# Inverting the chunk triangles: substitution down to 16x16 blocks, one more merge level on TensorE, pools in another order

## The chip, the core and the metric

The kernel runs on one core of a Trainium2 chip. The metric is the device time of one execution in microseconds, the median of several runs. One core has five engines that each work through a queue of their own, in order: TensorE (PE, with its weight loads as PEld), VectorE (DVE), ScalarE (ACT), GpSimd (POOL) and SyncE (SP, which here only issues transfers). They meet through semaphores. Transfers between device memory and the core's SBUF go through 16 DMA engines.

## The reference

One layer of a diffusion block over 1024 latent tokens and 256 context tokens, width 1024, all in float32. The part that matters here is the gated delta rule: 4 heads of width 128, both directions in time, in chunks. In each chunk a unit lower triangular system is solved:

```python
A = jnp.where(strict, jnp.einsum('nbhid,nbhjd->nbhij', kb, kc) * decay, 0.0)
rhs = jnp.concatenate([vc * bc[..., None], kb * jnp.exp(G)[..., None]], axis=-1)
sol = lax.linalg.triangular_solve(A + jnp.eye(CHUNK, dtype=A.dtype), rhs,
                                  left_side=True, lower=True, unit_diagonal=True)
u, w = sol[..., :dv], sol[..., dv:]
def step(S, xs):
    u_c, w_c, q_c, qk_c, k_c, gl = xs
    v_new = u_c - jnp.einsum('bhck,bhkv->bhcv', w_c, S)
    o = jnp.einsum('bhck,bhkv->bhcv', q_c, S) + jnp.einsum('bhij,bhjv->bhiv', qk_c, v_new)
    S = gl * S + jnp.einsum('bhck,bhcv->bhkv', k_c, v_new)
    return S, o
```

Around it stand, in this order, the modulated norm, one combined input projection (q, k, v with a short convolution, z, and four groups rq, rk, rv, rg for a second, retention branch of 4 heads with rotary positions), the norms and gates, the output projection, and a SwiGLU of inner width 2816.

## The kernel before

The 1280 tokens are 10 tiles of 128; the kernel takes 128 as the chunk of the delta rule too, so there are 10 tiles x 4 heads x 2 directions = 80 triangles of 128x128. Big products are made in three passes (hi x hi, hi x lo, lo x hi; lines L381 to L383, tile `tm`, 128x256 each). A scheduler fixes the order of every engine's queue ahead of the run; within it, a tile that takes an older tile's place in SBUF waits for that tile's last use. Tiles live in pools that are opened and closed like a stack, so what a pool lies upon depends on the order in which pools are opened.

The stages around the change:

- `token_major` projections of g 6 and 7 (rg) with their weights in pool W2; then R2 and W2 are closed and GP, GU and GI opened.
- `pre(t)` for each tile, in batches `BATCH = [[0,1,2,9],[3,8,4,7],[5,6]]`: on PE kk, the transpose qt and kq; on POOL the differences of decays `e` (L591, L593) and `sp` (L609); on ACT the exponentials (L595, L608); on DVE `ut` (L603) and `sp` (L605). The scaled triangles go out to device memory as `un` (L606), other operands of the scan as `sd` (L610).
- `invert(b)`: loads the 32x32 diagonal blocks of a batch as one row per block (`yr`, L624), copies them to L, straight for one direction on ACT (L631) and transposed for the other on DVE (L632), and inverts all blocks at once by 31 steps of substitution with two DVE operations each (L638, L640). X and its transpose XT (L642) go out as `xd` (L644).
- `solve(0)` and `solve(1)` are pre and invert of batches 0 and 1. Then come the v convolution (`conv_block`), whose result is transposed on PE (vT, L728), scaled on ACT into the only buffer `vt` (L731) and stored (L732), and `pre` of batch 2.
- `merge(b)`: loads U from `un` (L655), puts the inverted blocks over its diagonal blocks from `xd` (L659), and loads the transposed blocks into t64 (L660), which POOL has zeroed (L657). From the 32x32 inverses it makes those of 64 and then of 128 by products of the form -X1 A X2: 32x32 products (L679, L686, L689) with an eviction on DVE (L682) and copies on ACT (L692, L695), then 64x64 ones (L702, L706, L703, L708). The result is stored to `sd` (L710). U has one buffer, so a batch's load waits for the previous batch's store.
- invert(2) stands between merge(0) and merge(1). Beside the merges PE works on `tm` products of the next projections (fill).
- Then the scan, which loads its operands as `pk`; its steps (kS, r, Tr L792, vn, up L799) alternate between the directions. The rotary part of the second branch uses DVE (L398, L401) and POOL (L403).

Of the kernel before, what the change touches and what calls it, by code (L numbers as in the profile page):

```python
# [17 lines left out]
P = 128  # L18
D = 1024
# [18 lines left out]
def build(nc, tc, ap, dbg=None, stop=None, marks=None):  # L38
    root = ExitStack()
    V, S, G, T, SY = nc.vector, nc.scalar, nc.gpsimd, nc.tensor, nc.sync  # L40

    def pool(name, bufs=1, side=None, space=None):
        kw = {}
        if side is not None:
            kw["side"] = side
        if space is not None:
            kw["space"] = space
        if space is not DRAM:
            kw["reuse_waits"] = "tile"
# [8 lines left out]
    def close(p):  # L58
        p_close.pop(id(p)).close()
# [32 lines left out]
    def bank_b(name):  # L92
        return bank("pb", name)
# [67 lines left out]
    try:  # L161

        cc = const("cc", [P, KT, 2])
        ident = const("ident", [P, P])
# [118 lines left out]
        for gi, grp in enumerate(XGROUPS):  # L283
            n, t0 = len(grp), grp[0]
# [8 lines left out]
            sl = slice(t0 * P, (t0 + n) * P)  # L293
# [158 lines left out]
        ps = bank_b("G")  # L452
# [14 lines left out]
        ps = bank_b("GT")  # L467
# [145 lines left out]

        xds = {}

        def invert(b):

            nc_ = len(BATCH[b])
            nu = nc_ * H
            nb = 4 * nu  # L620
            xd = xds[b] = dr.tile([4 * nb, 1024], F32, tag="xd%d" % b, name="xd%d" % b)
            yr = GI.tile([P, 1024], F32, tag="yr", name="yr", bufs=1)
            for k in range(4):
                SY.dma_start(yr[k:2 * nb:4].rearrange("r (i j) -> r i j", j=32),  # L624
                             un[b][q32[k]].rearrange("i e u j -> (e u) i j")[:, :, q32[k]])
            L = GI.tile([P, 1024], F32, tag="L", name="L", bufs=3)
            X = GI.tile([P, 1024], F32, tag="X", name="X", bufs=2)
            G.memset(X, 0.0)
            G.memset(X[:, 0::33], 1.0)
            m = lambda t: t[:2 * nb].rearrange("p (i j) -> p i j", j=32)  # L630
            S.activation(L[:nb], yr[:nb], AF.Copy)  # L631
            V.tensor_copy(m(L)[nb:], yr[nb:2 * nb].rearrange("p (i j) -> p j i", j=32))  # L632
            for j in range(31):
                n = 31 - j
                tmp = GI.tile([P, 256], F32, tag="tmp%d" % b, name="tmp", bufs=2)
                t3 = tmp[:2 * nb, :n * (j + 1)].rearrange("p (i c) -> p i c", c=j + 1)
                sh = [2 * nb, n, j + 1]
                V.tensor_tensor(t3, bc(m(L)[:, j + 1:, j], sh, 2), bc(m(X)[:, j, :j + 1], sh, 1), ALU.mult)  # L638
                xs = m(X)[:, j + 1:, :j + 1]
                V.tensor_tensor(xs, xs, t3, ALU.subtract)  # L640
            XT = GI.tile([P, 1024], F32, tag="L", name="XT", bufs=3)
            V.tensor_copy(m(XT), X[:2 * nb].rearrange("p (i j) -> p j i", j=32))  # L642
            for i, x in enumerate((X[:nb], XT[nb:2 * nb], X[nb:2 * nb], XT[:nb])):
                SY.dma_start(xd[i * nb:(i + 1) * nb], x)  # L644

        def blocks(b):

            nu = len(BATCH[b]) * H
            nb = 4 * nu

            def blk(dram, k):
                return dram.rearrange("(u b) (i j) -> b i u j", b=4, j=32)[k]

            uu = GM.tile([P, 2, len(BATCH[b]), H, P], F32, tag="U", name="U%d" % b, bufs=1)
            SY.dma_start(uu.rearrange("p e c h j -> p e (c h) j"), un[b])  # L655
            tt = GM.tile([P, 2, nu, 64], F32, tag="t64", name="t64", bufs=1)
            G.memset(tt, 0.0)  # L657
            for k in range(4):
                SY.dma_start(uu[q32[k]].rearrange("p e c h j -> p (e c h) j")[:, :, q32[k]], blk(xds[b][:2 * nb], k))  # L659
                SY.dma_start(tt[q32[k]].rearrange("p e u j -> p (e u) j")[:, :, (k % 2) * 32:(k % 2) * 32 + 32],  # L660
                             blk(xds[b][2 * nb:], k))
            return uu, [uu[:, 1 - d] for d in range(2)], [tt[:, d] for d in range(2)]

        def merge(b):

            uu, ub, t64 = blocks(b)
            nu = len(BATCH[b]) * H
            q = q32
            u = [x.rearrange("p c h j -> p (c h) j") for x in ub]
            t = t64  # L670
# [3 lines left out]
            three = lambda ps, sl, w: ps[sl].rearrange("p (n j) -> p n j", j=w)  # L674
            ps1 = bank_b("m1")
            for n in range(nu):
                for d, p, a, bb in pairs:
                    ca = (a % 2) * 32
                    T.matmul(ps1[q[bb], n * 32:n * 32 + 32], u[d][q[a], n, q[bb]], t[d][q[a], n, ca:ca + 32],  # L679
                             start=True, stop=True)  # L680
            xt1 = GM.tile([P, 16, 32], F32, tag="xt1", name="xt1", bufs=1)
            V.tensor_scalar(xt1.rearrange("p n j -> p (n j)")[:, :nu * 32], ps1[:, :nu * 32], -1.0, None, ALU.mult)  # L682
            ps2, ps3 = bank_b("m1"), bank_b("m1")
            for n in range(nu):
                for d, p, a, bb in pairs:
                    T.matmul(ps2[q[a], n * 32:n * 32 + 32], xt1[q[bb], n, :], u[d][q[bb], n, q[bb]],  # L686
                             start=True, stop=True)
                    if p == d:
                        T.matmul(ps3[q[bb], n * 32:n * 32 + 32], u[d][q[bb], n, q[bb]], xt1[q[bb], n, :],  # L689
                                 start=True, stop=True)  # L690
            for d, p, a, bb in pairs:
                S.activation(u[d][q[a], :, q[bb]], three(ps2[:, :nu * 32], q[a], 32), AF.Copy)  # L692
                if p == d:
                    ca = (a % 2) * 32
                    S.activation(t[d][q[bb], :, ca:ca + 32], three(ps3[:, :nu * 32], q[bb], 32), AF.Copy)  # L695
            halves = [(0, slice(0, 64), slice(64, 128)), (1, slice(64, 128), slice(0, 64))]
            for n0 in range(0, nu, 8):
                ps1, ps2 = bank_b("m2"), bank_b("m2")
                xt2 = GM.tile([P, 8, 64], F32, tag="xt2", name="xt2", bufs=1)
                for n in range(8):  # L700
                    for d, A, B in halves:
                        T.matmul(ps1[B, n * 64:n * 64 + 64], u[d][A, n0 + n, B], t[d][A, n0 + n, :], start=True, stop=True)  # L702
                V.tensor_scalar(xt2.rearrange("p n j -> p (n j)"), ps1, -1.0, None, ALU.mult)  # L703
                for n in range(8):
                    for d, A, B in halves:
                        T.matmul(ps2[A, n * 64:n * 64 + 64], xt2[B, n, :], u[d][B, n0 + n, B], start=True, stop=True)  # L706
# [789 lines left out]
```

## Time and profile before

| | us |
|---|---|
| median of 3 runs (lowest, highest) | 1504.32 (1503.76, 1508.56) |
| the profiled execution | 1499.94 |
| its span | 1498.2 |
| PE busy | 1405.7 |
| DVE busy | 978.5 |
| POOL busy | 638.6 |
| ACT busy | 607.0 |

The profile is of one execution. Its rows are read as follows. A row of a group says line, engine, operation, written tile <- read tiles, shapes, the count, then the busy time with the mean of one in ns, then the idle time of the engine just before these instructions with what ended most of it. A row of the timeline says start and duration in us, engine, line and operation, and in brackets the idle time before it with what ended it. In the table by stretches, each engine has its busy time and its count; PEclk is TensorE's granted clock as a share of full speed, the mean of which over this execution was 0.974. The trace keeps two records for one 32x32 product in float32.

### The profile page before, as it was taken

The numbers are of one execution on the slowest core, as the hardware profiler recorded it, in microseconds if no ns is written. First come the engines' busy times: TensorE is split into PE (matmuls) and PEld (weight loads), VectorE is DVE, ScalarE is ACT, GpSimd is POOL, SyncE is SP. The second block draws the span as 40 slices with busy tenths as digits, with TensorE's granted clock in tenths as the row PEclk, the third lists the DMA queues.
The fourth block names the chain that finished last, engine by engine and source line by source line (L and its number), as shares of the span: only waits on it lengthen the run. The fifth ranks groups of instructions, "written<-read, shape, count | busy, mean of one in ns | idle before, by whom it ended". The sixth has DMA issues, their size and how long they took to land.

```text
span 1498.2 us, 24215 instructions
## 1 busy us (share of the span) xinstructions
PE 1405.7 (94%) x8927; PEld 1210.8 (81%) x8927; DVE 978.5 (65%) x1926; ACT 607.0 (41%) x1267; POOL 638.6 (43%) x589
## 2 busy tenths in 40 slices
PE   6899999987898899998799899989999999999997
PEld 2898888976888899988678688878888888788886
DVE  5966695279778345678767786646555555658477
ACT  5733653365451121235544433223333333445445
POOL 0310101387124243224326578989555553325322
PEclk9899999997999999999999999999999999999999
DMA  8555685478597756985742256665222231785863
GB/s 329 197 175 164 207 239 167 143 234 267 147 276 213 227 170 252 370 334 204 246 147 106 86 191 223 240 238 204 105 106 106 106 141 68 237 281 188 295 217 113
DMA packets 171703, 298.16 MB, mean 199 GB/s; under 512 B 43368, under 2 KB 93752, under 8 KB 166208
## 3 DMA queue, kind: packets, MB, share of 16 engines
q1 hardware_dynamic: 119424, 251.07, 48.9%
q10 hardware_dynamic: 49360, 36.88, 8.0%
q0 software_dynamic: 2800, 8.65, 1.6%
q8 instruction: 70, 1.15, 0.3%
q14 instruction: 49, 0.40, 0.1%
HBM read 206.60 MB, written 89.96 MB: 198 GB/s over the span
## 4 chain that ended last, share of the span: by engine, by line
PE 64%; DVE 12%; DMA 10%; POOL 5%; issue 4%; ACT 3%; SPq 1%; ACTq 0%; POOLq 0%; DVEq 0%
PE ffn L1187 8%; PE ffn L1186 8%; PE ffn L1185 8%; PE tm L383 4%; PE tm L382 4%; PE tm L381 4%; PE fo L1313 3%; PE fo L1312 3%; PE fo L1311 3%; PE b L484 2%; PE b L486 2%; PE b L485 2%; PE op L1044 2%; PE op L1046 2%; PE op L1045 2%
## 5 line engine op out<-in xcount | busy, mean ns | idle before, releaser
L381 PE MATMUL tm<-whi,hhi 128*128 128x256 f32 (+1 forms) x704 | 203.9, 292 | 8.7 <-ACT whi L319 4.3
L382 PE MATMUL tm<-wlo,hhi 128*128 128x256 f32 (+1 forms) x704 | 204.5, 292 | 3.1 <-DVE wlo L320 3.1
L383 PE MATMUL tm<-whi,hlo 128*128 128x256 f32 (+1 forms) x704 | 204.4, 293 | 0.0
L381 PEld LDWEIGHTS tm<-whi,hhi 128*128 128x128 f32 x704 | 137.4, 196 | 11.1 <-ACT whi L319 5.4
L382 PEld LDWEIGHTS tm<-wlo,hhi 128*128 128x128 f32 x704 | 138.0, 196 | 5.8 <-DVE wlo L320 3.6
L1185 PE MATMUL ffn<-t,whi 128*128 128x512 f32 x352 | 137.7, 392 | 4.0 <-ACT whi L319 3.0
L383 PEld LDWEIGHTS tm<-whi,hlo 128*128 128x128 f32 x704 | 137.6, 196 | 2.2 <-issue 0.9
L1187 PE MATMUL ffn<-t,wlo 128*128 128x512 f32 x352 | 137.5, 392 | 1.1 <-DVE wlo L320 1.1
L1186 PE MATMUL ffn<-t,whi 128*128 128x512 f32 x352 | 137.8, 392 | 0.5 <-DVE t L1080 0.5
L319 ACT ACTIVATE whi<-wraw 128x512 fp32r<-128x512 f32 (+2 forms) x98 | 75.2, 772 | 132.0 <-PE ffn L1186 77.6
L320 DVE TENSOR_TENSOR wlo<-ws,whi 128x512 fp32r<-128x512 f32 x88 | 94.4, 1073 | 50.1 <-ACT whi L319 50.0
L319 ACT ACTIVATE whi<-ws 128x512 fp32r<-128x512 f32 x88 | 55.6, 631 | 170.6 <-PE ffn L1186 120.1
L320 DVE TENSOR_TENSOR wlo<-wraw,whi 128x512 fp32r<-128x512 f32 (+2 forms) x92 | 100.5, 1094 | 35.6 <-ACT whi L319 35.3
L1312 PE MATMUL fo<-wlo,ahi 128*128 128x512 f32 x308 | 120.0, 390 | 0.8 <-DVE wlo L320 0.8
L1311 PE MATMUL fo<-whi,ahi 128*128 128x512 f32 x308 | 119.3, 390 | 0.7 <-ACT ahi L319 0.7
L1313 PE MATMUL fo<-whi,alo 128*128 128x512 f32 x308 | 118.8, 389 | 0.0
L1185 PE MATMUL ffn<-b,whi 128*128 128x512 f32 x264 | 103.7, 393 | 3.8 <-ACT whi L319 3.8
L1187 PE MATMUL ffn<-b,wlo 128*128 128x512 f32 x264 | 103.7, 393 | 1.6 <-DVE wlo L320 1.6
L1186 PE MATMUL ffn<-b,whi 128*128 128x512 f32 x264 | 103.5, 392 | 0.0
L484 PE MATMUL b<-hhi,whi 128*128 128x512 f32 (+1 forms) x256 | 95.5, 373 | 2.2 <-ACT y L488 2.2
L485 PE MATMUL b<-hlo,whi 128*128 128x512 f32 (+1 forms) x256 | 95.1, 372 | 0.0
L486 PE MATMUL b<-hhi,wlo 128*128 128x512 f32 (+1 forms) x256 | 94.8, 370 | 0.0
(422 smaller groups left out, 3495.3 us busy)
## 6 DMA issues: line engine op xcount, KB each, us to landing
adaw<-ada_w SPq DMA_DIRECT2D x48, 512.0 KB, 5.6
pk<-sd SPq DMA_DIRECT2D x16, 1536.0 KB, 9.7
wraw<-wfi SPq DMA_DIRECT2D x44, 512.0 KB, 3.5
ar<-ad SPq DMA_DIRECT2D x33, 512.0 KB, 6.5
w<-wfo SPq DMA_DIRECT2D x22, 512.0 KB, 3.5
wd<-tw SPq DMA_DIRECT2D x11, 1024.0 KB, 4.8
ad<-act SPq DMA_DIRECT2D x20, 512.0 KB, 4.7
raw<-wd SPq DMA_DIRECT2D x20, 512.0 KB, 5.0
```

The costliest lines, as they stand in the source:

```text
L319: S.activation(hi, raw, AF.Copy)
L320: e.tensor_tensor(lo, raw, hi.bitcast(F32), ALU.subtract)
L381: T.matmul(o, hhi[:, k, tsl], whi[:, k % 4, :], start=(k == 0), stop=False)
L382: T.matmul(o, hhi[:, k, tsl], wlo[:, k % 4, :], start=False, stop=False)
L383: T.matmul(o, hlo[:, k, tsl], whi[:, k % 4, :], start=False, stop=(k == KT - 1))
L484: T.matmul(o, whi[:, k, :], hh, start=(k == 0), stop=False)
L1185: T.matmul(o, whi[:, k, :], xhi(xn, slice(0, 4), k), start=(first and k == 0), stop=False, **kw)
L1186: T.matmul(o, whi[:, k, :], xlo(xn, slice(0, 4), k), start=False, stop=False, **kw)
L1187: T.matmul(o, wlo[:, k, :], xhi(xn, slice(0, 4), k), start=False, stop=(k == 3), **kw)
L1311: T.matmul(po[g][i], ahi[:, ts], whi, start=(j == 0 and not kw), stop=False, **kw)
L1312: T.matmul(po[g][i], ahi[:, ts], wlo, start=False, stop=False, **kw)
L1313: T.matmul(po[g][i], alo[:, ts], whi, start=False, stop=(j == FH - 1), **kw)
```

## The change

Five things are edited.

1. Substitution runs only inside the two 16x16 diagonal blocks of each 32x32 block: 15 steps, each on both blocks at once. Rows of L, X and yr are 1056 long, so that a view `halved` with a stride of 528 reaches both blocks.
2. Each merge begins with a new level from 16 to 32: POOL multiplies the off-diagonal 16x16 blocks into `off`, with a factor `half` (1 or 0 by partition) that keeps only the right rows (L683); PE multiplies `off` with the transposed blocks (L688), ACT evicts with a minus (nw, L691), PE makes the two products for the block and its transpose (L697, L701), and DVE adds them to DT and D (L703, L704). ACT copies the finished 32x32 blocks into U and t64 (L706, L708).
3. The inverted blocks are loaded into tiles of their own, D and DT (L664, L665), no longer over U and t64.
4. `half`, `off` and t64 are made once, ahead of merge(0), not per merge.
5. The pools are opened in the order GI, GU, GP; GP and GU are closed before GM is opened, behind pre of batch 2. Before, GM was opened ahead of that pre, beside all three.

The loads of yr and un, the store of xd and the later merge levels stay; their lines move (L624 to L627, L644 to L649, L655 to L660, L679 to L715, L682 to L718, L792 to L831 and so on).

```diff
+        GI = pool("gi")
+        GU = pool("gu")
         GP = pool("gp")
-        GU = pool("gu")
-        GI = pool("gi")
...
+        halved = lambda x: x.rearrange("p (s y) -> p s y", y=528)[:, :, :512].rearrange("p s (i j) -> p s i j", j=32)[:, :, :, :16]
...
-            S.activation(L[:nb], yr[:nb], AF.Copy)
-            V.tensor_copy(m(L)[nb:], yr[nb:2 * nb].rearrange("p (i j) -> p j i", j=32))
-            for j in range(31):
-                n = 31 - j
-                tmp = GI.tile([P, 256], F32, tag="tmp%d" % b, name="tmp", bufs=2)
-                t3 = tmp[:2 * nb, :n * (j + 1)].rearrange("p (i c) -> p i c", c=j + 1)
-                sh = [2 * nb, n, j + 1]
-                V.tensor_tensor(t3, bc(m(L)[:, j + 1:, j], sh, 2), bc(m(X)[:, j, :j + 1], sh, 1), ALU.mult)
-                xs = m(X)[:, j + 1:, :j + 1]
-                V.tensor_tensor(xs, xs, t3, ALU.subtract)
...
+            S.activation(Lh[:nb], yh[:nb], AF.Copy)
+            V.tensor_copy(Lh[nb:2 * nb], yh[nb:2 * nb].rearrange("p s i j -> p s j i"))
+            Lh, Xh = Lh[:2 * nb], Xh[:2 * nb]
+            for j in range(15):
...
+                tmp = GI.tile([P, 128], F32, tag="tmp%d" % b, name="tmp", bufs=2)
+                t4 = tmp[:2 * nb, :2 * n * (j + 1)].rearrange("p (s i c) -> p s i c", s=2, c=j + 1)
+                sh = [2 * nb, 2, n, j + 1]
+                V.tensor_tensor(t4, bc(Lh[:, :, j + 1:, j], sh, 3), bc(Xh[:, :, j, :j + 1], sh, 2), ALU.mult)
+                xs = Xh[:, :, j + 1:, :j + 1]
+                V.tensor_tensor(xs, xs, t4, ALU.subtract)
...
-            tt = GM.tile([P, 2, nu, 64], F32, tag="t64", name="t64", bufs=1)
-            G.memset(tt, 0.0)
+            dd = GM.tile([P, 2, nu, 32], F32, tag="D", name="D", bufs=1)
+            dt = GM.tile([P, 2, nu, 32], F32, tag="DT", name="DT", bufs=1)
             for k in range(4):
-                SY.dma_start(uu[q32[k]].rearrange("p e c h j -> p (e c h) j")[:, :, q32[k]], blk(xds[b][:2 * nb], k))
-                SY.dma_start(tt[q32[k]].rearrange("p e u j -> p (e u) j")[:, :, (k % 2) * 32:(k % 2) * 32 + 32],
-                             blk(xds[b][2 * nb:], k))
-            return uu, [uu[:, 1 - d] for d in range(2)], [tt[:, d] for d in range(2)]
+                SY.dma_start(dd[q32[k]].rearrange("p e u j -> p (e u) j"), blk(xds[b][:2 * nb], k))
+                SY.dma_start(dt[q32[k]].rearrange("p e u j -> p (e u) j"), blk(xds[b][2 * nb:], k))
+            return uu, dd, dt
...
+            nw = []
+            for d in range(2):
+                cols = slice(16 - 16 * d, 32 - 16 * d)
+                for k in range(4):
+                    G.tensor_scalar(off[q[k], d, :nu, cols], u[d][q[k], :, 32 * k + cols.start:32 * k + cols.stop],
+                                    half[q[k], d:d + 1], 1.0, ALU.mult, ALU.mult)
+                ps = bank_b("m0")
+                for n in range(nu):
+                    for k in range(4):
+                        T.matmul(ps[q[k], n * 32:n * 32 + 32], off[q[k], d, n, :], t32[d][q[k], n, :],
+                                 start=True, stop=True)
+                w = GM.tile([P, 16, 32], F32, tag="nw%d" % d, name="nw", bufs=1)[:, :nu]
+                S.activation(full(w), ps[:, :nu * 32], AF.Copy, scale=-1.0)
+                nw.append(w)
+            for d in range(2):
+                ps2, ps3 = bank_b("m0"), bank_b("m0")
+                for n in range(nu):
+                    for k in range(4):
+                        T.matmul(ps2[q[k], n * 32:n * 32 + 32], nw[d][q[k], n, :], u32[d][q[k], n, :],
+                                 start=True, stop=True)
+                for n in range(nu):
+                    for k in range(4):
+                        T.matmul(ps3[q[k], n * 32:n * 32 + 32], u32[d][q[k], n, :], nw[d][q[k], n, :],
+                                 start=True, stop=True)
+                V.tensor_tensor(full(t32[d]), full(t32[d]), ps3[:, :nu * 32], ALU.add)
+                V.tensor_tensor(full(u32[d]), full(u32[d]), ps2[:, :nu * 32], ALU.add)
+                for k in range(4):
+                    S.activation(u[d][q[k], :, q[k]], u32[d][q[k]], AF.Copy)
+                    if k // 2 == d:
+                        S.activation(t[d][q[k], :, (k % 2) * 32:(k % 2) * 32 + 32], t32[d][q[k]], AF.Copy)
...
-                    ca = (a % 2) * 32
-                    T.matmul(ps1[q[bb], n * 32:n * 32 + 32], u[d][q[a], n, q[bb]], t[d][q[a], n, ca:ca + 32],
+                    T.matmul(ps1[q[bb], n * 32:n * 32 + 32], u[d][q[a], n, q[bb]], t32[d][q[a], n, :],
...
-                    T.matmul(ps2[q[a], n * 32:n * 32 + 32], xt1[q[bb], n, :], u[d][q[bb], n, q[bb]],
+                    T.matmul(ps2[q[a], n * 32:n * 32 + 32], xt1[q[bb], n, :], u32[d][q[bb], n, :],
...
-        GM = pool("gm")
         for t in BATCH[2]:
             pre(t)
         checkpoint("pre2")
+        close(GP)
+        close(GU)
+        GM = pool("gm")
...
+        half = GM.tile([P, 2], F32, tag="half", name="half", bufs=1)
+        V.tensor_reduce(half[:, 0:1], ident.rearrange("p (k j) -> p k j", j=32)[:, :, 0:16], mybir.AxisListType.XY, ALU.add)
+        V.tensor_scalar(half[:, 1:2], half[:, 0:1], -1.0, 1.0, ALU.mult, ALU.add)
+        off = GM.tile([P, 2, 16, 32], F32, tag="off", name="off", bufs=1)
+        G.memset(off, 0.0)
+        tt = GM.tile([P, 2, 16, 64], F32, tag="t64", name="t64", bufs=1)
+        G.memset(tt, 0.0)
         merge(0)
         SY.dma_start(rope, ap["rope"])
         invert(2)
...
         checkpoint("rgz")
         close(GM)
         close(GI)
-        close(GU)
-        close(GP)
```

How the queues stand now, at the places where the order moves. In the rows, a name with a number is a tile and its running number, `x2` two rows alike; m_4274 and m_4191 are PSUM tiles of the first level of merge 0.

SP, the loads of merge 0, before: U's load and then the blocks from xd_3086 (batch 0) stand among the last stores of pre (un_2857 and sd, batch 2).

```order
L606 DMA un_2857<-ut 128x512 x2
L655 DMA U_4262<-un_2855 128x4096
L610 DMA sd<-sp 128x1024
L586 DMA gw<-grow_d 128x512
L742 DMA rope<-rope 128x1280
L610 DMA sd<-sp 128x1024
L660 DMA t_4264<-xd_3086 32x32x32 x4
L606 DMA un_2857<-ut 128x512
L659 DMA U_4262<-xd_3086 32x32x32 x4
```

SP, the same loads after:

```order
L606 DMA un_2857<-ut 128x512
L610 DMA sd<-sp 128x1024
L606 DMA un_2857<-ut 128x512
L610 DMA sd<-sp 128x1024
L627 DMA yr<-un_2857 16x32x32 x2
L660 DMA U_4175<-un_2855 128x4096
L664 DMA D<-xd_3086 32x32x32
L665 DMA DT<-xd_3086 32x32x32
```

U's load has moved behind all stores of pre and behind the yr loads of invert(2), which read un_2857.

PE at the start of merge 0 after the change, behind the fill (`tm`). Before, 78 `tm` stood between the last kq and the first product of merge 0, a single pair of L679; now 166 stand between the last kq and the first of L688, and 39 more, with four single L688 among them, before the rest:

```order
L383 MATMUL tm<-whi,hlo 128x256
L688 MATMUL m_4191<-DT,off 32x32
L688 MATMUL m_4262<-DT,off 32x32
L688 MATMUL m_4191<-DT,off 32x32 x61
L688 MATMUL m_4262<-DT,off 32x32 x61
L697 MATMUL m_4329<-D,nw 32x32 x64
L701 MATMUL m_4330<-nw,D 32x32 x64
L697 MATMUL m_4467<-D,nw 32x32 x64
L701 MATMUL m_4468<-nw,D 32x32 x64
L715 MATMUL m_4605<-DT,U_4175 32x32
```

The three products of the new level follow each other without fill; behind the first L715 come 24 `tm`, then the other 63. Between merges 0 and 1 stand 137 `tm` now (116 before), between merges 1 and 2 116 (136 before).

SP at the start of the scan, before: four loads of `pk` stand ahead of the loads of batch 2.

```order
L644 DMA xd_4526<-XT 32x1024 x2
L537 DMA pk_5527<-sd 128x2048
L537 DMA pk_5529<-sd 128x2048
L537 DMA pk_5559<-sd 128x2048
L537 DMA pk_5571<-sd 128x2048
L660 DMA t_4902<-xd_4526 32x16x32 x4
```

SP there after the change:

```order
L660 DMA U_4920<-un_2856 128x4096
L665 DMA DT<-xd_4857 32x16x32 x4
L664 DMA D<-xd_4857 32x16x32 x4
L660 DMA U_5601<-un_2857 128x2048
L537 DMA pk_6452<-sd 128x2048
L537 DMA pk_6454<-sd 128x2048
L537 DMA pk_6484<-sd 128x2048
```

The `pk` loads have moved behind U of batch 2; on PE the first Tr of the scan stands behind the 105 `tm` that follow merge 2, where before steps 0 and 1 stood among fill. On POOL the eight L683 of merge 0 stand ahead of rotary work (L403), and on DVE the whole substitution of batch 2 ahead of the first add L703 of merge 0. kk of the first tiles stands ahead of 189 `tm` of g 6 and 7 now, behind them before.

More of the change, by code (lines that the diff above doesn't have):

```diff
@@ L621, in invert @@
             xd = xds[b] = dr.tile([4 * nb, 1024], F32, tag="xd%d" % b, name="xd%d" % b)
-            yr = GI.tile([P, 1024], F32, tag="yr", name="yr", bufs=1)
+            yr = GI.tile([P, 1056], F32, tag="yr", name="yr", bufs=1)
             for k in range(4):
-                SY.dma_start(yr[k:2 * nb:4].rearrange("r (i j) -> r i j", j=32),
+                SY.dma_start(yr[k:2 * nb:4, :1024].rearrange("r (i j) -> r i j", j=32),
                              un[b][q32[k]].rearrange("i e u j -> (e u) i j")[:, :, q32[k]])
-            L = GI.tile([P, 1024], F32, tag="L", name="L", bufs=3)
@@ L627, in invert @@
[L627 removed]
+            L = GI.tile([P, 1056], F32, tag="L", name="L", bufs=3)
+            X = GI.tile([P, 1056], F32, tag="X", name="X", bufs=2)
             G.memset(X, 0.0)
[L629 to L640 removed]
@@ L641, in invert @@
-            XT = GI.tile([P, 1024], F32, tag="L", name="XT", bufs=3)
-            V.tensor_copy(m(XT), X[:2 * nb].rearrange("p (i j) -> p j i", j=32))
+            G.memset(X[:, 0:1024:33], 1.0)
+            m = lambda t: t[:2 * nb, :1024].rearrange("p (i j) -> p i j", j=32)
+            yh, Lh, Xh = halved(yr), halved(L), halved(X)
+            S.activation(Lh[:nb], yh[:nb], AF.Copy)
+            V.tensor_copy(Lh[nb:2 * nb], yh[nb:2 * nb].rearrange("p s i j -> p s j i"))
+            Lh, Xh = Lh[:2 * nb], Xh[:2 * nb]
@@ new lines, in invert @@
+            for j in range(15):
+                n = 15 - j
+                tmp = GI.tile([P, 128], F32, tag="tmp%d" % b, name="tmp", bufs=2)
[4 more added lines that the diff above has]
+                V.tensor_tensor(xs, xs, t4, ALU.subtract)
@@ L643, in invert @@
+            XT = GI.tile([P, 1056], F32, tag="L", name="XT", bufs=3)
+            V.tensor_copy(m(XT), X[:2 * nb, :1024].rearrange("p (i j) -> p j i", j=32))
             for i, x in enumerate((X[:nb], XT[nb:2 * nb], X[nb:2 * nb], XT[:nb])):
-                SY.dma_start(xd[i * nb:(i + 1) * nb], x)
+                SY.dma_start(xd[i * nb:(i + 1) * nb], x[:, :1024])
         def blocks(b):
@@ L662, in blocks @@
-            return uu, [uu[:, 1 - d] for d in range(2)], [tt[:, d] for d in range(2)]
+                SY.dma_start(dd[q32[k]].rearrange("p e u j -> p (e u) j"), blk(xds[b][:2 * nb], k))
+                SY.dma_start(dt[q32[k]].rearrange("p e u j -> p (e u) j"), blk(xds[b][2 * nb:], k))
+            return uu, dd, dt
         def merge(b):
-            uu, ub, t64 = blocks(b)
+            uu, dd, dt = blocks(b)
             nu = len(BATCH[b]) * H
             q = q32
-            u = [x.rearrange("p c h j -> p (c h) j") for x in ub]
@@ L670, in merge @@
-            t = t64
+            u = [uu[:, 1 - d].rearrange("p c h j -> p (c h) j") for d in range(2)]
+            u32, t32, t = [dd[:, 1 - d] for d in range(2)], [dt[:, d] for d in range(2)], [tt[:, d, :nu] for d in range(2)]
+            three = lambda ps, sl, w: ps[sl].rearrange("p (n j) -> p n j", j=w)
+            full = lambda x: x.rearrange("p n j -> p (n j)")
+            nw = []
[12 more added lines that the diff above has]
+                nw.append(w)
@@ L673, in merge @@
             pairs = [(d, p) + ((2 * p, 2 * p + 1) if d == 0 else (2 * p + 1, 2 * p)) for p in range(2) for d in range(2)]
-            three = lambda ps, sl, w: ps[sl].rearrange("p (n j) -> p n j", j=w)
             ps1 = bank_b("m1")
```

2 lines of the change are left out of this document (1 added, 1 removed).

## The prediction

> **What bounds the kernel now.** I read the page first (busy time, then the row of slices), then a table by stage around the change, then TensorE's gaps there in the timeline, and last the chain of work and the groups by line for prices.
>
> ```profile
> PE 1405.7 (94%) x8927; PEld 1210.8 (81%) x8927; DVE 978.5 (65%) x1926; ACT 607.0 (41%) x1267; POOL 638.6 (43%) x589
> PE   6899999987898899998799899989999999999997
> core 0: us, PE busy (x) PEld busy (x) DVE busy (x) ACT busy (x) POOL busy (x), PEclk, DMA share, GB/s
> 287.40:359.50 72.10, 62.38 (x373) 54.32 (x371) 56.68 (x138) 45.32 (x102) 58.45 (x80) 0.95 0.75 237
> 359.50:403.40 43.90, 34.56 (x225) 31.06 (x225) 38.26 (x88) 22.96 (x54) 12.39 (x18) 0.85 0.61 180
> 403.40:434.60 31.20, 29.00 (x232) 28.47 (x230) 24.50 (x66) 16.94 (x42) 9.31 (x13) 0.94 0.83 248
> 434.60:463.50 28.90, 26.70 (x573) 24.73 (x573) 17.32 (x47) 9.92 (x15) 7.88 (x14) 0.89 0.84 231
> 463.50:514.10 50.60, 42.54 (x701) 40.98 (x701) 33.32 (x88) 7.91 (x13) 18.57 (x34) 0.90 0.73 213
> 514.10:548.70 34.60, 33.85 (x467) 32.70 (x468) 11.86 (x34) 6.39 (x12) 14.10 (x31) 1.00 0.64 202
> ```
>
> TensorE is busy for 94% of the span, so the time is its work plus its gaps. The six stretches are: pre(0) and pre(1) up to the v convolution; that convolution; pre(2); merge 0; merge 1; merge 2. For each I call lost: the stretch less PE's busy time, plus busy time by (1 less granted clock). That is 9.7 + 3.1 = 12.8 us, 9.3 + 5.2 = 14.5, 2.2 + 1.7 = 3.9, 2.2 + 2.9 = 5.1, 8.1 + 4.3 = 12.4 and 0.8: some 50 us, more than which no faster inversion can give back. In the first two stretches VectorE is busy for 79% and 87%, the highest after PE. What PE waited for there and later:
>
> ```profile
> 365.42 2.51 PE L728 MATMUL vT<-ident,y 128*128 128x128 f32 x10 [3.37 <-DVE ut L603]
> 402.75 0.66 PE L728 MATMUL vT<-ident,y 128*128 128x128 f32 x4 [2.39 <-ACT vt L731]
> 433.87 0.38 PE L381 MATMUL tm<-whi,hhi 128*128 128x256 f32 x1 [1.85 <-ACT whi L319]
> 480.83 1.28 PE L679 MATMUL m<-t,U 32*32 32x32 f32 x128 [3.38 <-issue]
> 491.17 0.43 PE L689 MATMUL m<-xt,U 32*32 32x32 f32 x14 [2.77 <-DMA U<-xd]
> 532.14 0.75 PE L679 MATMUL m<-t,U 32*32 32x32 f32 x64
> ```
>
> The waits are of two kinds: on VectorE and ScalarE ahead of merge 0, on transfers (U<-un, U<-xd) at merge 1; merge 2 has none.
>
> **The change, part by part.** *The substitution.* Its price on VectorE comes from these groups, the first two over all forms, the others one form each:
>
> ```profile
> L640 DVE TENSOR_TENSOR X<-X,tmp 128x31 f32<-128x31 f32 (+23 forms) x93 | 38.6, 415 | 2.4
> L638 DVE TENSOR_TENSOR tmp<-L,X 128x31 f32<-128x31 f32 (+23 forms) x93 | 35.0, 376 | 3.2 <-ACT L L631 1.0
> L638 DVE TENSOR_TENSOR tmp<-L,X 128x31 f32<-128x31 f32 x4 | 0.8, 196 | 1.1 <-ACT L L631 1.0
> L638 DVE TENSOR_TENSOR tmp<-L,X 128x256 f32<-128x256 f32 x2 | 0.9, 426 | 0.1
> ```
>
> One inversion costs (38.6 + 35.0)/3 = 24.5 us. The two single forms give a line: (426 - 196)/(256 - 31) = 1.02 ns an element above 164 ns fixed. Fifteen steps on two blocks are 30 operations over 2 x 2 x 680 = 2,720 elements: 4.9 + 2.8 = 7.7 us, or 8.8 when raised as the old sum (62 x 0.164 + 10,912 x 0.00102 = 21.3) falls short of 24.5. VectorE is relieved of 47 us in three inversions, nearly all of it beside PE's work. What comes free can only be the part of 12.8 + 14.5 = 27.3 us lost ahead of pre(2) for which VectorE, or POOL behind it, was late. Two things in the way do not change:
>
> ```profile
> 281.82 2.80 POOL L591 TENSOR_SCALAR e<-gw,nG 128x128 f32<-128x128 f32 x8 [42.01 <-DMA rd<-res]
> L731 ACT ACTIVATE vt<-vT,svy x40: 349/367/385, 360.3 to 415.4; 128x128 f32<-128x128 f32 x40
> DMA to landing us min/median/max: 2.4/4.3/5.2
> ```
>
> The v convolution's vT goes through one vt buffer, twelve times in 55 us, each with a store of 4.3 us before the buffer is free. So I count the second stretch's 14.5 as staying, and of the first 12.8 some 11 as free, helped by the pools: GP no longer waits for both old pools, kk of the first tiles stands ahead of the 189 products of g 6 and 7, and POOL's idle 42 us before its first e can be used. Term: **-11**, ends 0 and -27.
>
> *The new level on PE.* It adds, for 16, 16 and 8 blocks, 2 directions x 4 quarters x 3 products = 960 products of 32x32, of which the trace makes two records each (L679: 160 products, 320 records), so 1,920. From the rows of L679 above, 64 records more take 1.28 - 0.75 = 0.53 us, 8.3 ns each: 15.9 us. It is PE's own time, with nothing beside it. Ends: 1.28/128 = 10 ns, 19 us; and below, nothing reduces it. Term: **+16**. The Trainium skill ("TensorE: Matmul & The Clock Gate", "Wait — 56ns, not 53.3ns?") says that matmuls never start less than about 25 ns apart however small they are; by it the term would be an estimated 24 us for 960 or 48 for 1,920. The rows disagree, since 128 records, or 64 products, took 1.28 us, 10 or 20 ns each, so this rule gets no chance of its own.
>
> Between L688 and L697 PE has no other work in its order: the eviction nw stands on the path once in each merge, by the rows below 0.58 us and the start behind it, say 0.8. The adds L703/L704 (12 of about 0.68 on VectorE, 8 us in all) and the ACT copies L706/L708 (36 in all) have 24 and more fill products of 0.12 us behind the first L715. If those don't cover, the price doubles. Term: **+2.5**, ends 1 and 6.
>
> ```profile
> L692 ACT ACTIVATE U<-m 32x512 f32<-32x512 f32 x8 | 4.7, 584 | 22.0 <-PE m L689 21.9
> L682 DVE TENSOR_SCALAR xt<-m 128x512 f32<-128x512 f32 x2 | 1.4, 683 | 0.9 <-PE m L679 0.9
> 448.03 0.28 PE L383 MATMUL tm<-whi,hlo 128*128 128x256 f32 x1
> 448.15 0.28 PE L381 MATMUL tm<-whi,hhi 128*128 128x256 f32 x1
> L591 POOL TENSOR_SCALAR e<-gw,nG 128x128 f32<-128x128 f32 x80 | 41.4, 533 | 63.7 <-DMA rd<-res 42.0 <-DVE sp L605 12.5 <-DVE ut L603 5.0
> ```
>
> *Merge 0's data.* Before, U, U's blocks and t64 were loaded while pre(2) ran; merge 0 waited for nothing. Now GM is opened over the closed GP and GU, and U's load stands in SP's queue behind pre(2)'s last stores and invert(2)'s yr loads, which need the landing of the un store.
>
> ```profile
> 421.68 1.05 PE L583 MATMUL kq<-qc,kc 128*128 128x128 f32 x8
> 427.72 6.44 SPq L660 DMA_DIRECT2D t<-xd  x4
> 434.82 3.55 SPq L659 DMA_DIRECT2D U<-xd  x4
> 437.73 0.34 DVE L605 SCALAR_TENSOR_TENSOR sp<-kq,ab,e 128x128 f32<-128x128 f32 x1
> 440.72 6.17 DMA un<-ut
> 462.36 1.17 PE m L706 x32
> 465.33 5.24 DMA sd<-U
> 470.69 10.05 DMA U<-un
> 484.27 7.49 DMA U<-xd
> ```
>
> From the last kq at 421.7 to the landing of un at 446.9 are 25 us; 1 for yr's issue, 10 for the load of U (the row for batch 1, of the same size), 2.1 for four off on POOL at L591's 0.53: 38. In front of the first L688 PE has kq and 166 fill products of 0.117: 20.5. The gap would be 18. But 10 us of that chain were the two issues of xd blocks on SP at 427.7 and 434.8, ahead of pre(2)'s stores, and they now stand behind; I take 8 off for them, since part ran beside other links. Off both ways the ends are 3 (if pre(2)'s e and exp shorten too) and 18. Term: **+10**. The 1.85-us wait on whi at 433.9 lies under it: **-2**. A wait of this length has its price in the clock as well: in the ten us behind such waits the granted clock was low.
>
> ```profile
> 360.00:370.00 10.00, 5.63 (x21) 4.07 (x20) 9.83 (x26) 4.88 (x12) 7.28 (x12) 0.53 0.85 298
> 490.00:500.00 10.00, 6.92 (x209) 6.61 (x210) 4.78 (x16) 3.42 (x6) 2.36 (x5) 0.66 0.06 19
> ```
>
> At 0.53 and 0.66 they lost 2.6 and 2.4 us of work, which the term of 10 holds. The Trainium skill (the same page, "PE_HAM") says that an idle window of about 3.4 us halves the clock for about as long; the rows agree (3.37 idle, then 0.53), and by it the estimated price is 1.7 us a wait, no other sum.
>
> *Merges 1 and 2.* Merge 1 lost 12.4, because U's load starts when merge 0's sd store has read U (465.3 to 470.6), takes 10, and then the xd blocks land on it (to 491.8). D and DT have tiles of their own, so that last link goes. From L706 at 462.4 to U at 480.7 are 18.4, with off 20.5, against 137 fills (16.1) and L706 (1.2): a wait of 3.2 and 2.3 of clock, 5.5. Term: **-7**, ends 0 and -12. Merge 2 had 0.8 lost; its off now stands on the chain, and its fill falls from 136 to 116 products (13.6 us): **+2**, ends 0 and 6.
>
> *Scan and queues.* Steps 0 and 1 stood amid fill; now the pk loads stand behind batch 2's U in SP's queue and the first Tr after the last fill, so nothing hides their evictions: **+2**, ends 0 and 6. POOL's off stands ahead of the rotary L403 and invert(2) on VectorE ahead of merge 0's adds; in the merges' stretches the table has VectorE at 55% and POOL at 36%, so a late instruction has room to catch up: nothing, up to 5. The factors half and the memsets of off and t64 run once, while merge 0 waits for U; without that wait they would cost about one eviction.
>
> Sum: 16 + 2.5 - 11 + 10 - 2 - 7 + 2 + 2 = **+12.5**. The profiled run took 1499.94 us (span 1498.2), 4.4 below the median of 1504.32; so 1512.4 against the one, 1516.8 against the other.
>
> **Rivals.** *Faster.* VectorE was the limit of both stretches ahead of pre(2), and the vt ring merely followed it. For it speaks VectorE's 87% in the second; against it the wait on vt at 402.8, where ScalarE and a store were late. Then -27 instead of -11, and with the pre(2) chain shortened by its lighter queues merge 0 waits 3 instead of 10: 12.5 - 16 - 7 = -10.5, 1493.8. It decides once more than 23.5 of those 27.3 us go, or 16.5 with the short wait. *No change.* Half of the second stretch (7) comes free and merge 0's wait is 5: 12.5 - 7 - 5 = +0.5, 1504.8. *Nothing comes free in front.* POOL's e and the vt ring keep PE waiting whatever VectorE does: +11, 1527.8.
>
> **How the numbers follow.** Forecast 0.47, nothing free 0.11, no change 0.17, faster 0.25. Measurement can tell about 0.3%, 4.5 us. The two slower cases hold 0.58, no change 0.17. The forecast's own range, merge 0's wait from 3 to 16, is 1510 to 1523. Leaving a tenth out on each side cuts the faster case at its middle, 1494, and reaches to the case with nothing free, 1528.
>
> **What would show it.** L643/L645 at 30 operations and near 9 us an inversion. Right: a gap of about 8 us in PE ahead of L688 that U<-un or off ends; L688, L697 and L701 with 1,920 records in 16 us; merge 1's gap near 3; the first Tr after the last fill. Wrong: vt's forty copies in clearly under 55 us (the ring was not the limit), no gap at L688, POOL's first e still after 42 idle us, or PE's gaps between 287 and 403 as large as now.

## The result, and the profile after

The changed kernel took 1559.84 us (median of 4 runs, 1558.17 to 1565.09) against 1504.04 us before: a ratio of 1.0399, with a 95% interval of 1.0368 to 1.0429. It is slower, as forecast, by 56 us instead of 12.5, and lies far outside the range of 1494 to 1528. The profiled execution took 1565.09 us (span 1563.3).

From the page after: the busy times, the row of granted clocks by slice, and the queue that carries the engines' instructions (packets, MB, share).

```profile
PE 1444.6 (92%) x10847; PEld 1245.5 (80%) x10847; DVE 943.8 (60%) x1844; ACT 632.7 (40%) x1311; POOL 638.9 (41%) x612
PEclk9899999999988799999989989999999999999999
q8 instruction: 85, 1.39, 0.4%
```

The last row on the page before:

```profile
q8 instruction: 70, 1.15, 0.3%
```

PE has 1,920 more records and is busy for 38.9 us more: 20 ns for each new record, where the forecast had 8.3. In that are older products which ran at a lower clock; the new products' own groups have 29.9 us, 16 ns each:

```profile
L688 PE MATMUL m<-DT,off 32*32 32x32 f32 x640 | 9.2, 194 | 6.2 <-issue 3.5 <-DMA DT<-xd 1.6 <-POOL off L683 1.0
L697 PE MATMUL m<-D,nw 32*32 32x32 f32 x640 | 10.0, 225 | 8.0 <-issue 8.0
L701 PE MATMUL m<-nw,D 32*32 32x32 f32 x640 | 10.7, 229 | 12.0 <-issue 12.0
```

The page also has 15 more instruction packets, 0.24 MB, so 16 KB each. The kernel has 28,064 instructions for 24,215: 3,849 more, and 3,849/15 is 257 to a packet of 16 KB, 64 bytes an instruction.

The table by stretches after: the v convolution, from the last kq to the first L688, merge 0's new level and the 32-to-64 level, the rest up to merge 1, merge 1's new level, up to merge 2, merge 2's new level.

```profile
core 0: us, PE busy (x) PEld busy (x) DVE busy (x) ACT busy (x) POOL busy (x), PEclk, DMA share, GB/s
359.40:404.40 45.00, 33.23 (x224) 29.40 (x223) 29.68 (x71) 24.87 (x57) 14.87 (x22) 0.90 0.74 220
...
424.50:448.70 24.20, 20.87 (x160) 20.27 (x159) 8.68 (x26) 10.52 (x20) 9.24 (x16) 0.93 0.89 275
448.70:485.60 36.90, 26.84 (x983) 25.33 (x983) 15.67 (x49) 9.36 (x15) 9.48 (x20) 0.68 0.41 76
485.60:521.50 35.90, 35.24 (x558) 34.15 (x557) 11.63 (x33) 7.92 (x12) 12.90 (x25) 1.00 0.65 201
521.50:545.00 23.50, 13.86 (x783) 12.46 (x784) 3.64 (x10) 5.27 (x9) 7.50 (x17) 0.66 0.07 21
545.00:587.36 42.36, 39.60 (x691) 37.67 (x689) 12.99 (x36) 11.25 (x18) 15.85 (x34) 0.95 0.51 163
587.36:596.20 8.84, 4.61 (x383) 4.25 (x382) 1.10 (x4) 3.25 (x8) 2.24 (x5) 0.86 0.10 33
```

The stretches that hold the new level stand out: PE is busy for 73%, 59% and 52% of them, at clocks of 0.68, 0.66 and 0.86, and no other engine is near its limit (in merge 1 the busiest is POOL with 32%, and the DMA engines are at 7%). What PE waits for, its timeline shows in merge 0 (fill and pieces of fewer records left out):

```profile
448.73 0.21 PE L688 MATMUL m<-DT,off 32*32 32x32 f32 x2 [1.59 <-DMA DT<-xd]
...
456.01 1.51 PE L688 MATMUL m<-DT,off 32*32 32x32 f32 x146
459.54 1.03 PE L688 MATMUL m<-DT,off 32*32 32x32 f32 x100 [2.02 <-issue]
...
463.54 1.55 PE L697 MATMUL m<-D,nw 32*32 32x32 f32 x100 [2.62 <-issue]
...
467.00 1.55 PE L701 MATMUL m<-nw,D 32*32 32x32 f32 x100 [1.52 <-issue]
...
470.45 1.55 PE L697 MATMUL m<-D,nw 32*32 32x32 f32 x100 [1.52 <-issue]
...
474.73 1.51 PE L701 MATMUL m<-nw,D 32*32 32x32 f32 x97 [2.35 <-issue]
```

The gaps stand in the middle of a product's run, not at its ends, and nothing that the profile knows ends them ("issue"); the only semaphore waits on record at L688 and L697 are of 51 ns, and L701 has none. They come every 128 records (100, 4 in pieces and 24): with as many weight loads, 256 instructions, just one packet of 16 KB. From 459.54 to 474.73 four such blocks took 15.2 us: 3.5 to 4.3 us each, 3.8 in the mean, or 30 ns a record. The queue of instructions keeps the same pace: in the 23.5 us of merge 1's new level it moved 6 packets.

```profile
q8 instruction: 6, 0.10, 1.8%
```

In the waits of PE over the merges (line, releaser: us, times, longest):

```profile
PE m L701 <- issue: 12.0, 6, 2.3
PE m L697 <- issue: 8.0, 4, 2.6
PE m L688 <- issue: 3.5, 2, 2.0
PE m L722 <- issue: 2.0, 1, 2.0
```

That is 25.5 us in 13 waits (the last one, L722, stands in the level behind the new one), beside which the waits for the data (DT<-xd 1.6 at merge 0) are small. No product of the level waited for the eviction nw. From the first record of its unbroken run to the fill behind it the level lasts 20.3, 20.3 and 8.5 us in the three merges, 49 in all.

### The profile page after: what moved, and what is told of

Its sections match the earlier page's. It is cut to its first block, busy times and chain, and to the rows that moved or that the text cites. A ratio compares the mean times of both kernels' runs of the same rounds, so it can differ in the third digit from the quotient of the medians.

```text
span 1563.3 us, 28064 instructions
## 1 busy us (share of the span) xinstructions
PE 1444.6 (92%) x10847; PEld 1245.5 (80%) x10847; DVE 943.8 (60%) x1844; ACT 632.7 (40%) x1311; POOL 638.9 (41%) x612
## 4 chain that ended last, share of the span: by engine, by line
PE 53%; POOL 5%; DMA 5%; DVE 4%; issue 4%; ACT 2%; SPq 0%; ACTq 0%; POOLq 0%; DVEq 0%
PE ffn L1231 7%; PE ffn L1230 6%; PE ffn L1229 6%; PE fo L1355 4%; PE fo L1357 4%; PE fo L1356 4%; PE tm L381 2%; PE tm L382 2%; PE tm L383 2%; PE op L1089 2%; PE op L1090 2%; PE op L1088 2%; DMA wd<-tw 1%; PE Tr L836 1%; POOL ws L1202 1%
## 5 line engine op out<-in xcount | busy, mean ns | idle before, releaser
L320 DVE TENSOR_TENSOR wlo<-wraw,whi 128x512 fp32r<-128x512 f32 (+2 forms) x92 | 103.7, 1129 | 45.8 <-ACT whi L319 45.5
```

What stands on the lines that cost most here:

```text
L320: e.tensor_tensor(lo, raw, hi.bitcast(F32), ALU.subtract)
```

## The experiments

The theory from here on: PE consumes the new level's 32x32 products faster than their instructions arrive; a block of 256 takes about 3.8 us to come. Rivals: the products' own time in the array (at full or half clock), the waits on evictions, and the loads behind the new order of pools.

**As many instructions, twice the work.** Edit, alike for the three products of the level:

```diff
-T.matmul(ps[q[k], n * 32:n * 32 + 32], off[q[k], d, n, :], t32[d][q[k], n, :],
+T.matmul(ps[q[k], n * 32:min(n + 2, nu) * 32], off[q[k], d, n, :],
+         full(t32[d][q[k], n:min(n + 2, nu), :]), ...
```

> Every product of the new level is made twice as wide (64 columns instead of 32, the second half overwritten by the next product), with the same number of instructions. Theory 1, PE waits for its instructions (a block of 256 in about 3.6 us whatever they do): the gaps ended by 'issue' shrink as the products grow, a block takes 3.5 to 4.0 us, and the time stays within 8 us of the changed kernel's, 1555 to 1568. Rival, the products' own time in the array: 16 us more at full clock, up to 39 at half clock, 1576 to 1599. Rival, transfers ahead of the merges: 1560, with the gaps unchanged.

1554.33 us, ratio 1.0328 (1.0280 to 1.0376): no slower than the changed kernel, and 0.7 us below the lower end of what was expected. The timeline of PE, merge 0:

```profile
458.54 2.29 PE L688 MATMUL m<-DT,off 32*32 32x64 f32 x146
461.44 1.54 PE L688 MATMUL m<-DT,off 32*32 32x64 f32 x96 [0.62 <-issue]
...
465.72 1.54 PE L697 MATMUL m<-D,nw 32*32 32x64 f32 x96 [2.34 <-issue]
...
469.45 1.54 PE L701 MATMUL m<-nw,D 32*32 32x64 f32 x96 [1.79 <-issue]
...
473.72 1.54 PE L697 MATMUL m<-D,nw 32*32 32x64 f32 x96 [2.33 <-issue]
```

Twice the columns, and blocks still begin 3.7 and 4.3 us apart. The clock was another one, too: over the level of merge 0, 20.5 us in both kernels, it was 0.62 in the changed kernel and 1.00 here (the third column from the end). At merge 1 it was 0.66 in the changed kernel's 23.5 us and 1.00 in the 23.5 us here.

```profile
455.50:476.00 20.50, 10.46 (x760) 9.66 (x763) 12.12 (x41) 5.59 (x9) 4.23 (x9) 0.62 0.20 52
```

```profile
458.50:479.00 20.50, 11.91 (x765) 11.04 (x765) 12.09 (x42) 5.21 (x9) 4.23 (x9) 1.00 0.19 50
523.10:546.60 23.50, 14.98 (x788) 13.51 (x789) 4.12 (x11) 5.38 (x9) 7.51 (x17) 1.00 0.07 21
```

So neither array work nor the clock sets the level's time: the clock was higher with the wider products, and that bought nothing inside the level.

**Half the instructions, the same work.** The wide products, for even n only:

```diff
-for n in range(nu):
+for n in range(0, nu, 2):
     for k in range(4):
-        T.matmul(ps[q[k], n * 32:n * 32 + 32], off[q[k], d, n, :], t32[d][q[k], n, :],
+        T.matmul(ps[q[k], n * 32:n * 32 + 64], off[q[k], d, n, :], full(t32[d][q[k], n:n + 2, :]),
```

> In the new level only every second product is made, each 64 columns wide (for the odd units with the even unit's left operand, so the output is not the reference's): the array does the same number of columns, PE gets half the instructions, 480 products for 960. Theory 1, the price is one of instructions (27 us for each 960 records): the time falls by 22 to 28 us, to 1527 to 1538, q8 moves 7 to 8 packets less. Rival, the price is the array's work, its clock or the evictions around it: within 6 us of the kernel with all products twice as wide, 1548 to 1560.

1530.22 us, ratio 1.0196 (1.0161 to 1.0230): 24 us below the wide one and 30 below the changed kernel, with 8 instruction packets more than before instead of 15.

```profile
q8 instruction: 78, 1.28, 0.3%
```

Together the two runs separate what the changed kernel mixes: work doubled at equal instructions, nothing; instructions halved at equal work, half the loss. 960 records fewer gave 24 us, 25 ns each. These two runs alone would also fit a fixed cost of each product in the array; against that stand the rows, in which 100 records follow each other in 1.0 to 1.6 us and the rest of the time lies in one gap per 256 instructions.

**The instructions spread.** The fill products of g 8 and 9 are put between those of the level by an order edge, once three behind every eight and once twelve behind every thirty-two:

```diff
+def feed(n, last):
+    if n % 2:                      # second kernel: n % 8 == 7, and four steps
+        with tc.issue_after(last.ins):
+            next(zs, None)         # three products of g 8 or 9
 for n in range(nu):
     for k in range(4):
-        T.matmul(...)
+        last = T.matmul(...)
+    feed(n, last)
```

> In the new level three wide products of g 8 and 9 stand behind every eight 32x32 products, by an order edge; the same work, spread. Theory 1: a block of 256 instructions then holds about 3.4 us of work, so the gaps ended by 'issue' in the level nearly go; merge 0's level takes about 25 us instead of 20 alone plus 16.8 of fill. The waits ahead of merges 0 and 1 lose their cover (no fill is left for them, some 15 to 20 us each), so the time is 1545 to 1575. Rival, the products or their evictions are slow by themselves: merge 0's level takes 37 us and the time is 1590 or more.

> As the kernel with three wide products behind every eight small ones, but in lumps: twelve wide ones behind every thirty-two. If the half clock in that kernel came from PE's changes between small and wide products, there are a quarter as many here, the clock in the level returns above 0.8 and the time falls below 1640; gaps ended by 'issue' may come back, up to 1 us each. If the clock was low for another reason (the idle 24 us ahead of each merge), it stays near 0.5 in the level and the time near 1700.

1709.97 us, ratio 1.1364 (1.1312 to 1.1416), and 1624.28 us in a single run. The totals say little: the waits ahead of merges 0 and 1 lost their cover, 23 to 24 us at one place ahead of merge 0 and 14 to 15 us at one ahead of merge 1. In the level both have not one gap ended by "issue". The second kernel there (PE's timeline, each followed by twelve wide products):

```profile
453.13 0.75 PE L707 MATMUL m<-DT,off 32*32 32x32 f32 x64
455.43 0.75 PE L717 MATMUL m<-D,nw 32*32 32x32 f32 x64
457.72 0.75 PE L717 MATMUL m<-D,nw 32*32 32x32 f32 x64
460.01 0.75 PE L722 MATMUL m<-nw,D 32*32 32x32 f32 x64
```

Every 2.29 us come 64 small records and twelve wide products; these take 12 x 0.117 = 1.40, which leaves 0.89 for the 64, 14 ns each and not 26 to 30. A block of 256 instructions then lasts 3.9 us, and the instructions are in time. No product of the level waits for the eviction nw there either. The clock and the total of this kernel are as expected if changes between small and wide products keep the clock low. In the first kernel my expectation failed: the time is 135 us above its upper end, on the rival's side of 1590, and merge 0's level took 68 us (442 to 510), neither the theory's 25 nor the rival's 37. No product there waited for an eviction, which the rival needs. The level from 448.5 to 500 us:

```profile
448.50:500.00 51.50, 51.50 (x753) 40.06 (x752) 9.72 (x33) 7.95 (x14) 0.00 (x0) 0.50 0.08 22
```

PE counts as busy throughout and waits for nothing, but at a clock of 0.50 that did not rise once in 51 us; with a quarter as many changes between small and wide products it was 0.93 between 460 and 480 us. Why it stays low is not shown. The Trainium skill says ("TensorEngine Tiling (Array Packing)", "Key Properties") that a change of tiling mode drains TensorE, which would leave the array idle at each change; in these runs fewer changes went with the higher clock, and none shows a drain by itself.

**The change without its level.** Both kernels keep the new pools, D and DT, and leave the level out: one with 15 steps (16x16 inverses merged as if they were 32x32), one with the 31 steps of before.

```diff
-            nw = []
-            for d in range(2):
-                ...                    # off, L688, nw, L697, L701, the adds
             for d in range(2):
                 for k in range(4):
                     S.activation(u[d][q[k], :, q[k]], u32[d][q[k]], AF.Copy)
```

> As the changed kernel, but without the level from 16 to 32 (no off, no products, no adds; the 16x16 inverses alone are merged, so the output is not the reference's). Theory 1: the level's 48.7 us go, and a few more behind it: 1503 to 1512. Rival, the new order of pools and loads costs most of the 56 us: above 1530. If the shorter substitution frees PE ahead of the v convolution's end after all, this one is some 10 us below the kernel with 31 steps and no level; by theory 1 and the trace (last kq at 423.4 against 422.5) within 4.

> Substitution in 31 steps as before, no new level, but the new order of pools, the late GM, and D and DT in tiles of their own. Theory 1: the new level is the whole loss, so this one lies within 6 us of the kernel before, 1498 to 1510, below it if D and DT shorten the wait at merge 1 as the trace suggests (12.4 us lost there before). Rival, pools and loads: 1530 or more. Forecast's term of the substitution (-11): this one 11 us above the one with 15 steps and no level.

1507.52 us, ratio 1.0029 (0.9999 to 1.0059), and 1512.09 us, ratio 1.0056 (1.0031 to 1.0082). The second lies 2 us above what was expected. So the level is 1.0399 - 1.0029 = 3.7%, some 55 us, by the medians 52; from 31 to 15 steps the intervals overlap.

**The substitution alone, with the old pools.** The kernel before, with the halved views of the change and nothing else of it:

```diff
-for j in range(31):
-    n = 31 - j
+for j in range(15):
+    n = 15 - j
```

> The kernel before with the substitution of 15 steps alone: old pools, blocks loaded over U and into t64 as before, no new level (so the output is not the reference's). The two kernels without the level put the worth of the shorter substitution at 4.6 us (1507.5 against 1512.1): 1495 to 1501 here, and the pools and loads at 9. If the forecast's term holds with the old pools, 1488 to 1494. If the shorter substitution is worth something only behind the new pools, 1502 to 1506.

1504.08 us, ratio 1.0010 (0.9992 to 1.0028): worth nothing, and outside the 1495 to 1501 that I held likeliest. It lies in the range for a worth behind the new pools only, but that worth is not clear either, as the intervals of the two kernels above overlap. Its table for the two stretches ahead of pre(2), to be laid beside the first two rows of the prediction's:

```profile
287.40:359.50 72.10, 62.33 (x378) 54.40 (x376) 54.96 (x139) 45.51 (x104) 57.74 (x78) 0.98 0.75 236
359.50:403.40 43.90, 33.15 (x219) 29.36 (x220) 26.62 (x70) 21.51 (x54) 12.22 (x20) 0.88 0.72 210
```

VectorE went from 38.3 to 26.6 us in the second stretch; PE did no more work in the same time. By the prediction's measure PE lost 11.0 and 14.7 us in the two stretches, for 12.8 and 14.5 before. The copies into vt run from 360.2 to 414.8, as before.

**A second vt buffer,** in the kernel before and with the 15 steps:

```diff
-vt = CV.tile([P, 4, P], F32, tag="vt", name="vt", bufs=1)
+vt = CV.tile([P, 4, P], F32, tag="vt", name="vt", bufs=2)
```

> The kernel before with two vt buffers instead of one. If the ring of one buffer with its stores (15.0 us of waits on sd<-vt, forty copies in 55 us) holds the v convolution's stretch, PE's waits there (9.3 us idle, 14.5 lost) shrink: 1492 to 1500. If VectorE, 87% busy there with the 31 steps, takes over as the limit, 1500 to 1506, no change.

> The substitution of 15 steps with old pools and no new level, as before (its output is not the reference's), and two vt buffers. If the ring is what kept VectorE's relief from paying, the two together gain what neither does alone: 1486 to 1495, and at least 6 us below the kernel with two buffers and 31 steps. If PE's gaps in front come from elsewhere (e, qt, weights), 1498 to 1504 and within 4 us of the other.

1502.03 us, ratio 1.0004 (0.9987 to 1.0021), and 1492.53 us, ratio 0.9928 (0.9904 to 0.9952). Neither edit pays alone; both together gain 0.7%, about the 11 us that the forecast had for the substitution. The last kq (first and last start of the group) moved from 422.5 us to

```profile
L583 PE MATMUL kq<-qc,kc x64: 270/275/418, 302.0 to 403.5; 128*128 128x128 f32 x64
```

with the second buffer alone, and in the 43.9 us from 359.5 PE is busy for 37.8 us instead of 34.6. So the ring of one buffer did hold part of the v convolution's stretch, though the time of the kernel stayed. With both edits PE is busy there for 37.4 us, no more. The traces do not carry the rest: with both edits kq ends at 403.1 and the output projection begins at 738.1 us, against 738.5 with the buffer alone. In these two executions 4.6 of the 5.5 us between them lie in the feed-forward stage, which neither edit touches, and which took 432 to 439 us in the eleven profiles of this case. Where the 10 us between the medians come from stays open. Since the new level costs far more than that even at half its instructions, no version of the change is likely to fall below the kernel before; none was run with the second buffer.

## Why the prediction was wrong

- **The new level, +16 and +2.5: the step that failed.** It measured 46 us to the start of the output projection in the profiles (801.2 against 755.0 without it), 52 to 55 in the times. The arrival of the instructions is the cost that I put at nothing, without a reason: "PE's own time, with nothing beside it". I priced a record from the rows of 128 and 64 L679, at 0.53/64 = 8.3 ns, and took that for runs of 768 and 384 records. Those rows are at most one block of 256 instructions long, and no gap stands inside them. In the longer runs a block came every 3.8 us, 30 ns a record, and 23.5 us of the level were gaps ended by "issue". The products' own 30 us, for 16, went with the low clock and did not decide: at full clock, in the kernel with wide products, the blocks came no faster. "Below, nothing reduces it" and an upper end of 19 us fell with this step. The +2.5 for the eviction nw came to nothing, as no product waited for it.

  The 3.38 us in front of the row of 128 are no such gap, though the timeline has "issue" there as well. PE's queue of weight loads stood on a semaphore for 3.7 us from 477.1, and U<-un landed at 480.7 (470.69 + 10.05): I had rightly counted that wait as merge 1's transfers. The trace before did hold one gap of the new kind, in merge 1 behind 184 of the 192 records of L686 and L689, where no semaphore wait above 51 ns is on record. I left it out.

```profile
L679 PEldq EVENT_SEMAPHORE  x1: 3715/3715/3715, 477.1 to 477.1; - x1
495.35 0.27 PE L686 MATMUL m<-U,xt 32*32 32x32 f32 x3 [1.71 <-issue]
```

- **The page's rule that got no chance.** The floor of 25 ns a matmul (the Trainium skill, "TensorE: Matmul & The Clock Gate", "Wait — 56ns, not 53.3ns?") made an estimated 48 us of 1,920, which is near what came. As far as these runs show that is a coincidence: inside a block 64 records took 0.75 us, 12 ns each, so no such floor held here, and the total comes from the 3.8 us of a block of 128.
- **What the Trainium skill says of arrival** ("Runtime: NRT & Kernel Launch", "Instruction fetch mechanics"): blocks of 16 KiB, 256 instructions, fetched while the one before runs, and that crossing into the next is mostly hidden. The packets and the spacing of the gaps agree with the block; "hidden" holds for the 128x256 products of the fill, where 256 instructions last 15 us (128 x 0.117), and not for these, which use a block up in 1 to 2 us and then stand for 1.5 to 2.6.
- **The relief of VectorE, -11.** The price was right (9.0 us an inversion for 8.8 forecast):

```profile
L643 DVE TENSOR_TENSOR tmp<-L,X 128x30 f32<-128x30 f32 (+15 forms) x45 | 13.8, 306 | 1.2
L645 DVE TENSOR_TENSOR X<-X,tmp 128x30 f32<-128x30 f32 (+15 forms) x45 | 13.1, 292 | 1.1
```

  What it bought was nothing: the ratio with it alone is 1.0010, with an interval around 1. POOL's first e did move, from 281.8 to 254.0, and the first kk to 254.5, but the last kq came at 423.4 after 422.5. I let the vt ring hold the second stretch only. The vT of the v convolution and the pre tiles behind it follow one another in PE's order, so the ring may have held the end of both; that is argued and not shown, since a second buffer alone gained nothing. In its outcome the rival "nothing comes free in front" was the true case for this term.
- **Merge 0's data, +10 and -2.** From kq at 423.4 to L688 at 448.7 are 25.3 us against 20.5 of fill: 4.8. The chain did contract, as the lower end had it: the last sp (432.7) began 9.3 us behind the last kq, not 15 as before.
- **Merge 1, -7, merge 2 and scan, +4.** Merge 1's stretch ahead of L688 lost 0.7 us for 12.4, more than forecast. Pools, loads and D together cost 0.2 to 0.6% (1.0029 against 1.0010 with 15 steps, 1.0056 against the kernel before with 31): 3 to 8 us, where those terms gave 5. The first of the two is not clear of noise, as its intervals overlap.

The sum was 12.5; with 52 to 55 for the level, nothing for the relief and 3 for the rest it is 55 to 58, and 56 was measured. This is no test of the parts, since the level was itself taken as the difference of two of these kernels.

## What to carry to other kernels

Price a run of small instructions by the whole of a period, with the gaps that its rows show in brackets, and count instructions as well as work: on PE 256 of them, weight loads included, came about every 3.8 us here. A gap ended by "issue" inside a row of equal products, at equal distances, was arrival here; one at the head of a row can still be a wait on a semaphore, which the engine's queue shows. Arrival gaps went away with long products in between and shrank with fewer products, not with a faster clock. An engine that is 87% busy next to the waiting one need not be the limit: here its relief and a second buffer paid only together, 0.7%, by a path that the traces do not show.

## What the runs showed that was not expected

Alternating eight 32x32 products with three of 128x256 kept PE's granted clock at 0.50 for over 50 us of unbroken work; thirty-two with twelve let it rise to 0.93 and 1.00. Why is not shown. And in an otherwise equal kernel with twice the columns per product the clock over the level was 1.00 instead of 0.62 and 0.66, at no cost in time.
